# Three of the four products of the first layer's scale and shift in split float32r

## The chip, the cores and the metric

One core of one Trainium2 chip. The metric is the device time of one execution of the whole program in microseconds (us); the runs of the kernel before are given with their median.

## The reference, cut to what matters

Two layers of a diffusion backbone over 256 latent and 256 context tokens with 1024 features. Everything starts with a scale and a shift of the inputs, which come from a conditioning vector: one for the latent stream (`c`), one for the context stream (`c_ctx`).

```python
mod_l = (jax.nn.silu(c) @ lp['w_ada'] + lp['b_ada'])[:, None, :]
mod_c = jax.nn.silu(c_ctx) @ lp['w_ada'] + lp['b_ada']
sh1_l, sc1_l, g1_l, sh2_l, sc2_l, g2_l = jnp.split(mod_l, 6, axis=-1)
sh1_c, sc1_c, g1_c, sh2_c, sc2_c, g2_c = jnp.split(mod_c, 6, axis=-1)
hl = xl * (1 + sc1_l) + sh1_l
hc = xc * (1 + sc1_c) + sh1_c
pl = hl @ lp['w_in']
```

`w_ada` is 1024 x 6144 for each layer, `w_in` 1024 x 8704. For the first layer's first product, `sc1` and `sh1` of all 1024 features are needed, which are 2048 columns of `w_ada`.

## The kernel before, in words

Features lie on the 128 partitions, in 8 tiles of features; the 512 tokens of both streams lie side by side in the free dimension. Every large product is made of three float32r products: an operand is split into a high part (ScalarE rounds it to float32r, `split`, L155) and a low part (the rest, a subtraction on VectorE or, where told so, on GpSimd, `lo_of`, L152), and `mm3` (L162 to L164) adds high x high, high x low and low x high in PSUM. The weights come as a stream of blocks of 128 x 1024 (`wfetch`), each split into `whi` and `wlo`, tiles of which there are three each.

The program's start, in `run`, goes so:

- `c` and `c_ctx`, as columns (`cc`), go through silu.
- The scale (j = 1) and the shift (j = 0) of the first 512 features (half 0), then of the other 512 (half 1), come from `ada_half`, called four times in the order (1,0), (0,0), (1,1), (0,1), written here as (j, half). Each call has four pieces of weights of 128 x 2 x 512 (`adar`, 512 KB each, fetched in `ada_raw`). It takes two columns of `cc` as the stationary operand and lets a piece's 512 columns stream by in float32, over eight tiles of features: eight products, which the trace shows as 16 matmuls of L1205. The row of two streams x 512 is copied out of PSUM by ScalarE (`adarow`, L1207), turned into columns by four transposes (L1210), and VectorE adds the bias and writes `mod` (L1213).
- `first_h` makes the first product's moving operand from x, scale and shift: per tile of features and stream, ScalarE writes the high part `hh` (L1180), VectorE the exact value `hf` (L1182), and the low part `hl` is the difference, on VectorE for one stream and on GpSimd for the other. It is called once for each half of the features.
- The first three tiles of the first projection (`u`, stationary operands `wx`, `wx` and one `whi`) are begun with the first half of the features (`early_half`, 12 products a tile) and ended with the second half. The next tile is `uv`.

In between, the hyena filter's small network (`filter_hidden`, with a sine on VectorE and ScalarE) is worked on.

Order on each engine is set by a scheduler at build time, which places an instruction by the order of the program, by priority (`high_priority` moves the calls of `ada_half` and the second `first_h` ahead) and by free tiles. On the chip each engine then goes through its list in that order, and waits on semaphores. All fetches here are issued by SyncE.

Of the kernel before, what the change touches and what calls it, by code (L numbers as in the profile page):

```python
# [11 lines left out]
F32R = mybir.dt.float32r  # L12
I32 = mybir.dt.int32
AF = mybir.ActivationFunctionType
ALU = mybir.AluOpType
# [33 lines left out]
RS = -1024.0 / 27      # what the reciprocal square roots come multiplied with  # L49

# columns of the packed per-feature vectors of one layer
# [12 lines left out]
class Kernel:  # L64
# [48 lines left out]
    def pair(self, T, name):  # L113
        """high and low parts of [1024 features, T tokens]: one (hi, lo) for each tile of features"""
        if T == 512:
            a, b = self.big(F32R, name=name + "h"), self.big(F32R, name=name + "l")
            return [(a[:, k], b[:, k]) for k in range(KT)]
        t = self.big(F32R, [P, 2, KT, T], name=name)
        return [(t[:, 0, k], t[:, 1, k]) for k in range(KT)]

    # ---- work in the background: generators that go one step on after each tile of a projection,
    #      so that what a step waits for has been issued a tile earlier ----
# [43 lines left out]
    def mmx(self, out, a, b, start, stop):  # L166
        """as mm3, or one float32 product where the operands have not been split"""
        if isinstance(a, tuple):
            self.mm3(out, a, b, start, stop)
        else:  # L170
            self.nc.tensor.matmul(out, lhsT=a, rhs=b, start=start, stop=stop)
# [40 lines left out]
    def fill(self, n):  # L212
        """fetches up to n blocks of weights, and two more into a large tile"""
# [6 lines left out]
    def wblock(self, ahead=2):  # L220
        """the next block of the weight stream as (hi, lo); the blocks after it are asked for early"""
# [11 lines left out]
    def dense(self, h, T, name):  # L233
        """one tile of 128 output features: [P, T] in PSUM"""
# [12 lines left out]
    def dense_by_stream(self, h, T, n, name):  # L247
        """n tiles, all of one stream's products before the other's; the last stream goes by tile of features,
        as they come out of the normalisation"""
# [10 lines left out]
    def dense_by_feature(self, ws, os, h, c0, T):  # L260
        """several tiles at once, one tile of input features after the other"""
# [9 lines left out]
    def rsqrt(self, out, var, scale, shape, tag):  # L271
        """out = RS / sqrt(var * scale + EPS)"""
# [6 lines left out]
    def newton(self, x, a, t):  # L279
        """x = RS / sqrt(a): a seed from the exponent bits, a cubic step x' = x (r^2 - 10/3 r + 5) with r = a x^2,  # L280
        which leaves 8/3 times the next value, and a Newton step that takes it as it comes"""
# [14 lines left out]
    def sine(self, out, pre, b, freq):  # L296
        """out = sin(freq * (pre + b)), the argument brought into [-pi, pi]"""
# [12 lines left out]
    def bcast_cols(self, ps_out, cols):  # L310
        """ps_out[:, i*128+j] on every partition = cols[j, i] / D"""
# [7 lines left out]
    def filter_hidden(self, l):  # L319
        """hidden features of the filter's network, [HID, SEQ]: their high parts and, below, their low ones"""  # L320
# [24 lines left out]
    def start_filters(self, l):  # L345
        """starts the filters; self.inv: the inverse transform's table, [freq, parity, cos/sin, 128];
        self.fwd: the forward one's, [tok, (parity, cos/sin, 128)], in the first layer split into high and low parts"""
        if l == 0:
            self.specs = {}
            self.hyb = self.big(F32R, [P, 4, 2, 512], name="hyb")      # two filters' parts, the tokens', the table  # L350
# [7 lines left out]
    def filter_chain(self, l):  # L358
        """specs[quarter]: spectrum of the normalised filter plus the skip weight for 256 channels,
        [freq, freq tile, re/im, ch], and what is left to multiply with"""  # L360
# [18 lines left out]
    def filter_quarter(self, l, qd, wf, hk, spec):  # L379
        """The filter has its skip weight times its norm added to its first tap; its norm is divided out at the very end."""  # L380
# [8 lines left out]
        hk = v4(hk, "hk")                                      # [tok, fwd/bwd, parity, ch]  # L389
# [13 lines left out]
        sq = wf.rearrange("p (i c) -> p i c", i=4)           # its inputs are spent  # L403
# [5 lines left out]
        # per-channel norm, as columns  # L409
# [35 lines left out]
    def parts(self, dst, src, eng=None):  # L445
        """splits src [tok, parity, ch] into dst; returns the pair of parts for a parity"""
# [4 lines left out]
    def transform(self, l, out, zc, zs):  # L451
        """cosine sums of zc and sine sums of zs, both [tok, ch] by parity, into [freq, freq tile, cos/sin, ch].
        The second tile holds the frequencies mirrored: 255 - k, with the sine's sign turned."""
# [24 lines left out]
    def hyena_unit(self, l, qd, s, z, x0, hy):  # L478
        """long convolution of 256 channels of one stream"""
# [21 lines left out]
        y = next(self.ys)                                      # [freq, re/im, freq tile, ch]  # L501
# [5 lines left out]
        # what the even and what the odd tokens are made of  # L507
# [18 lines left out]
    def short_conv(self, l, u, ch, out, ns):  # L526
        """out = three-tap convolution along the tokens of each stream + bias"""
# [9 lines left out]
    def hyena(self, l, h, T):  # L537
        """units of the last quarter are left to what follows"""
# [26 lines left out]
    def pool_in(self, l, h, T, po):  # L565
        """window mean minus value, all channels"""
# [3 lines left out]
        for c in range(KT):  # L570
# [7 lines left out]
            # the sum of a window of `step` tokens; its range shrinks as the window grows  # L578
# [15 lines left out]
    def pool_out(self, l, po, T, half):  # L594
        """the groups' projections of one half of the channels, in place"""
# [82 lines left out]
    def keys(self, kf, sqs, kh):  # L678
        """normalises and rotates the keys, on the way into kh"""
# [31 lines left out]
    def query(self, hh, q, sq, qs, st, kh, vh, T):  # L711
        """the queries' norms, as columns; after a group of heads its rotation, and its heads are let go"""
# [24 lines left out]
    def head(self, hh, s, q, qs, kh, vh, T, shared):  # L737
        """attention of one head over one stream's queries; its output takes the queries' place"""
# [58 lines left out]
    def ln_tile_(self, st, m, o, eng=None):  # L797
        """tile m of the residual sum, o its product in PSUM. The deviations are taken from the
        mean of the first tile's features; the rest of the mean comes out at the end."""
# [35 lines left out]
    def ln_sums(self, st):  # L835
        """the sums over all but the last tile, on every partition"""
# [16 lines left out]
    def ln_finish_(self, st, outs, done=None, gap=1):  # L853
        """outs: (kind, destination, scale columns, shift columns), fed from the normalised value"""
# [3 lines left out]
        bc, a, t = st["bc"], st["acc"][:, 0], st["acc"][:, 1]      # the sums' place is free again  # L858
# [38 lines left out]
    def raw_pair(self, a, b):  # L897
        """high and low parts of a value before its normalisation, scaled by what follows it; two more columns: the scale, the shift"""
# [12 lines left out]
    def from_raw(self, o, rm):  # L911
        """the product with the normalised value from that with the raw one"""
# [8 lines left out]
    def fold(self, g, b, sc, sh):  # L921
        """(x*g+b)*sc+sh as one scale and one shift"""
# [68 lines left out]
    def layer(self, l, h, hc, xa):  # L991
# [74 lines left out]
        if ns == 1:  # L1066
# [4 lines left out]
            # the head of the next product goes by the raw value, so that it need not wait for the normalisation  # L1071
# [38 lines left out]
    def run(self):  # L1110
# [9 lines left out]
        th = self.const([P, KT, 2], "ccolt")  # L1120
        nc.scalar.activation(th, cc, AF.Tanh, scale=0.5)
        nc.vector.tensor_scalar(out=th, in0=th, scalar1=0.5, scalar2=0.5, op0=ALU.mult, op1=ALU.add)
        nc.vector.tensor_tensor(out=cc, in0=cc, in1=th, op=ALU.mult)
        x = self.big(F32, [P, KT, 512], name="x")
# [11 lines left out]
        # the first tiles of the first projection, from one half of their features after the other  # L1136
# [207 lines left out]
```

## Time and profile before

| | |
|---|---|
| time, median of 3 runs | 1757.83 us (1756.98 to 1757.92) |
| span of the profiled execution, first to last instruction | 1754.7 us |
| the median less that span | 3.1 us |
| TensorE busy | 1685.5 us, 96% of the span |
| VectorE, ScalarE, GpSimd busy | 1237.0, 711.8, 334.7 us |
| chain that ended last | PE 80%, DVE 12%, issue 3%, ACT 2%, POOL 1%, DMA 1% |

The profiled execution's own time is not given beyond its span; what lies around the span is taken as the difference to the median. PE is TensorE's matmuls, PEld its weight loads, DVE VectorE, ACT ScalarE, POOL GpSimd, SP SyncE. The chain is followed back from the last instruction to what released it. All that the change touches lies in the first 60 us.

### The profile page before, as it was taken

Reading aid. Unit: us, or ns where it says so; the run is one execution under the profiler, and the core shown is the slowest. Engines: PE = TensorE matmul, PEld = TensorE weight load, DVE = VectorE, ACT = ScalarE, POOL = GpSimd, SP = SyncE. Lnnn points to the kernel's source line nnn. Section 1 sums busy time; section 2 is a strip of 40 time slices with the busy share of each in tenths; the row PEclk is TensorE's granted clock in tenths of the full one; section 3 lists DMA queues with packets and bytes.
Section 4 is the critical chain, followed back from the end, with each engine's and each line's share of the span. In section 5 each row is a group of like instructions: output and inputs, shape, how many; then the busy total and the mean of one; then the engine's idle time right before and its main releaser. Section 6 shows DMA issues by size and latency. Waiting matters only on the chain.

```text
span 1754.7 us, 25630 instructions
## 1 busy us (share of the span) xinstructions
PE 1685.5 (96%) x9930; PEld 1458.4 (83%) x9930; DVE 1237.0 (70%) x2050; ACT 711.8 (41%) x1132; POOL 334.7 (19%) x314
## 2 busy tenths in 40 slices
PE   8999999999999999899999999989999999989996
PEld 2788887788888888788888877879899999979995
DVE  4778878655777765878865576499874785796665
ACT  3433333432454433342232222255353664554442
POOL 1143451001200000340000041156500210130011
PEclk9999999999999999999999999989999999999998
DMA  8422222444322344216666564134353535545552
GB/s 319 146 79 85 72 83 94 144 142 141 124 72 73 132 154 135 85 61 192 191 196 198 186 195 132 61 121 144 120 165 126 173 97 160 173 135 184 190 181 84
DMA packets 68769, 243.34 MB, mean 139 GB/s; under 512 B 8166, under 2 KB 8616, under 8 KB 68392
## 3 DMA queue, kind: packets, MB, share of 16 engines
q1 hardware_dynamic: 67192, 236.78, 41.2%
q0 software_dynamic: 1168, 4.72, 0.9%
q8 instruction: 78, 1.28, 0.3%
q14 instruction: 43, 0.35, 0.1%
q10 hardware_dynamic: 288, 0.21, 0.0%
HBM read 238.01 MB, written 1.05 MB: 136 GB/s over the span
## 4 chain that ended last, share of the span: by engine, by line
PE 80%; DVE 12%; issue 3%; ACT 2%; POOL 1%; DMA 1%; SPq 0%; ACTq 0%; DVEq 0%; POOLq 0%
PE f L163 7%; PE f L162 7%; PE f L164 7%; PE b L162 4%; PE b L163 4%; PE b L164 4%; PE g L164 4%; PE g L162 4%; PE g L163 4%; PE w L162 3%; PE w L164 3%; PE w L163 3%; DVE wlo L152 2%; PE ux L162 1%; PE q L162 1%
## 5 line engine op out<-in xcount | busy, mean ns | idle before, releaser
L155 ACT ACTIVATE whi<-raw 128x1024 fp32r<-128x1024 f32 x322 | 340.9, 1059 | 666.1 <-issue 128.5
L152 DVE TENSOR_TENSOR wlo<-raw,whi 128x1024 fp32r<-128x1024 f32 x311 | 400.1, 1287 | 218.0 <-ACT whi L155 216.5
L183 DVE SCALAR_TENSOR_TENSOR junk<-ada,silu 128x1024 bf16<-128x1024 f32 x128 | 158.3, 1237 | 79.4 <-DMA ada<-adat 78.5
L162 PE MATMUL f<-h2h,whi 128*128 128x512 f32 (+1 forms) x320 | 125.7, 393 | 0.9 <-DVE sg L957 0.9
L163 PE MATMUL f<-h2l,whi 128*128 128x512 f32 (+1 forms) x320 | 125.6, 393 | 0.0
L164 PE MATMUL f<-h2h,wlo 128*128 128x512 f32 (+1 forms) x320 | 125.6, 393 | 0.0
L829 POOL TENSOR_TENSOR y<-y,lncs 128x256 f32<-128x256 f32 (+2 forms) x12 | 21.7, 1836 | 419.9 <-ACT lncs L824 419.9
L162 PE MATMUL f<-h,whi 128*128 128x256 f32 x312 | 88.5, 284 | 6.7 <-DVE fraw L916 6.7
L162 PE MATMUL w<-a,whi 128*128 128x256 f32 (+1 forms) x284 | 90.8, 320 | 0.0
L164 PE MATMUL w<-a,wlo 128*128 128x256 f32 (+1 forms) x284 | 89.6, 315 | 0.0
L163 PE MATMUL w<-a,whi 128*128 128x256 f32 (+1 forms) x284 | 89.5, 315 | 0.0
L163 PE MATMUL f<-h,whi 128*128 128x256 f32 x312 | 88.3, 283 | 0.0
L164 PE MATMUL f<-h,wlo 128*128 128x256 f32 x312 | 88.2, 283 | 0.0
L164 PE MATMUL g<-hh,wlo 128*128 128x512 f32 x192 | 76.8, 400 | 0.0
L162 PE MATMUL g<-hh,whi 128*128 128x512 f32 x192 | 76.7, 399 | 0.0
L163 PE MATMUL g<-hl,whi 128*128 128x512 f32 x192 | 76.3, 398 | 0.0
L162 PEld LDWEIGHTS f<-h2h,whi 128*128 128x128 f32 x320 | 60.1, 188 | 15.2 <-DVE sg L957 1.1
L164 PEld LDWEIGHTS f<-h2h,wlo 128*128 128x128 f32 x320 | 60.1, 188 | 14.3
L163 PEld LDWEIGHTS f<-h2l,whi 128*128 128x128 f32 x320 | 60.1, 188 | 14.1
L162 PEld LDWEIGHTS f<-h,whi 128*128 128x128 f32 x312 | 59.4, 191 | 6.9 <-ACT y L895 6.9
L163 PEld LDWEIGHTS f<-h,whi 128*128 128x128 f32 x312 | 59.5, 191 | 0.0
L164 PEld LDWEIGHTS f<-h,wlo 128*128 128x128 f32 x312 | 59.4, 191 | 0.0
(478 smaller groups left out, 4990.8 us busy)
## 6 DMA issues: line engine op xcount, KB each, us to landing
raw<-wst SPq DMA_DIRECT2D x336, 512.0 KB, 3.6
ada<-adat SPq DMA_DIRECT2D x80, 512.0 KB, 3.9
adar<-ada SPq DMA_DIRECT2D x16, 512.0 KB, 10.2
qsw<-q POOLq DMA_DIRECT2D x16, 128.0 KB, 4.8
x<-x_t POOLq DMA_DIRECT2D x1, 2048.0 KB, 9.6
x<-x_t SPq DMA_DIRECT2D x1, 1024.0 KB, 11.4
x<-x_t SPq DMA_DIRECT2D x2, 512.0 KB, 10.2
silu<-c_row SPq DMA_DIRECT2D x2, 512.0 KB, 7.9
```

Of the source, the lines that this page charges most:

```text
L152: (eng or self.nc.vector).tensor_tensor(out=lo, in0=src, in1=hi.bitcast(F32), op=ALU.subtract)
L155: self.nc.scalar.activation(hi, src, AF.Copy)
L162: t.matmul(out, lhsT=ah, rhs=bh, start=start, stop=False)
L163: t.matmul(out, lhsT=ah, rhs=bl, start=False, stop=False)
L164: t.matmul(out, lhsT=al, rhs=bh, start=False, stop=stop)
L183: nc.vector.scalar_tensor_tensor(out=junk, in0=raw, scalar=1.0, in1=self.silu[:, s], op0=ALU.mult, op1=ALU.mult, accum_out=mod[:, s, m : m ...
L829: nc.gpsimd.tensor_tensor(out=y[:, a:b], in0=xa[:, a:b], in1=cb.to_broadcast([P, b - a, SEQ]), op=ALU.subtract)
```

## The change

Three of the four calls of `ada_half`, all but (1,0), get their weights split into float32r parts and a stationary operand of four columns: high parts of the two columns of `c` and their low parts (`ccolp`). Each of the eight tiles of features then takes two float32r matmuls (high and low part of the weights) instead of one float32 product. The four rows that come out are folded into two by the small products that turn rows into columns, whose moving operand is now `fold4` instead of a 2 x 2 identity; (1,0) uses `fold4` too, in its first two rows. The split pieces are `whi`/`wlo` tiles, from the same three of each as the weight stream's; of the four pieces of a call the third has its low part made on GpSimd, the others on VectorE. The small tile `ccolt` comes from the pool `t2`.

```diff
@@ run
-        th = self.const([P, KT, 2], "ccolt")
+        th = self.t2(name="ccolt")[:, : 2 * KT].rearrange("p (k s) -> p k s", s=2)
         nc.scalar.activation(th, cc, AF.Tanh, scale=0.5)
         nc.vector.tensor_scalar(out=th, in0=th, scalar1=0.5, scalar2=0.5, op0=ALU.mult, op1=ALU.add)
         nc.vector.tensor_tensor(out=cc, in0=cc, in1=th, op=ALU.mult)
+        cp = self.sb.tile([P, KT, 4], F32R, tag="ccolp", name="ccolp", bufs=1)
+        self.split(cp[:, :, 0:2], cp[:, :, 2:4], cc)
+        self.fold4 = self.const([4, 2], "fold4")
+        nc.vector.tensor_tensor(out=self.fold4, in0=self.ident[:4, 0:2], in1=self.ident[:4, 2:4], op=ALU.add)
+        cc = (cc, cp)
...
@@ ada_half
         o = self.aux(name="adar")
+        exact, parts = cc
+        n = 2 if (j, half) == (1, 0) else 4
         for kp in range(4):
+            if n == 2:
+                ws = (raws[kp],)
+            else:
+                ws = [self.sb.tile([P, 2, 512], F32R, tag=t, name=self.nm("a" + t), bufs=3) for t in ("whi", "wlo")]
+                self.split(*ws, raws[kp], nc.gpsimd if kp == 2 else None)
             for k in range(2):
-                nc.tensor.matmul(o[:2], lhsT=cc[:, 2 * kp + k], rhs=raws[kp][:, k], start=kp + k == 0, stop=kp + k == 4)
+                for i, w in enumerate(ws):
+                    nc.tensor.matmul(o[:n], lhsT=(exact if n == 2 else parts)[:, 2 * kp + k], rhs=w[:, k],
+                                     start=kp + k + i == 0, stop=kp + k == 4 and i == len(ws) - 1)
         row = self.t2(name="adarow")
-        nc.scalar.activation(row[:2], o[:2], AF.Copy)
+        nc.scalar.activation(row[:n], o[:n], AF.Copy)
         tp = self.aux([P, 4, 2], name="adat")
         for m in range(4):
-            nc.tensor.transpose(tp[:, m], row[:2, m * P : (m + 1) * P], self.ident[:2, :2])
+            nc.tensor.matmul(tp[:, m], lhsT=row[:n, m * P : (m + 1) * P], rhs=self.fold4[:n], start=True, stop=True)
```

Three places in the order of instructions matter. The first is TensorE's list from the filter's second product (`hf`) to the first product with a low part of the weights `wx`. Before:

```order
L336 MATMUL hf_25_163<-hf1h_134,hfs_92 128x256
L1205 MATMUL adar_249<-adar_220,ccol 2x512 x2
L1205 MATMUL adar_249<-adar_222,ccol 2x512 x2
L1205 MATMUL adar_249<-adar_224,ccol 2x512 x2
L1205 MATMUL adar_249<-adar_226,ccol 2x512 x2
L162 MATMUL u_234<-hh_88,wx_211 128x512
L163 MATMUL u_234<-hl_89,wx_211 128x512
L162 MATMUL u_235<-hh_88,wx_211 128x512
L163 MATMUL u_235<-hl_89,wx_211 128x512
L162 MATMUL u_236<-hh_88,whi_230 128x512
```

and in the change:

```order
L336 MATMUL hf_34_192<-hf1h_139,hfs_97 128x256
L162 MATMUL u_263<-hh_93,wx_240 128x512
L163 MATMUL u_263<-hl_94,wx_240 128x512
L162 MATMUL u_264<-hh_93,wx_240 128x512
L163 MATMUL u_264<-hl_94,wx_240 128x512
L164 MATMUL u_263<-hh_93,wx_240 128x512
```

The product of (1,1), four pieces, stood ahead of the first tiles of `u`, and that of (0,1) directly behind these five; now both come later, in parts, among the products of `u`.

The second place is VectorE's list from the low parts of the first two weight blocks (`wx`) to the second half's `hf`; `mod_72` is the scale, `mod_71` the shift. Before:

```order
L152 TENSOR_TENSOR wx_211<-raw_212,wx_211 128x1024
L1213 SCALAR_TENSOR_TENSOR mod_72<-adat_260,vecs 128x4 x2
L152 TENSOR_TENSOR wx_211<-raw_216,wx_211 128x1024
L1213 SCALAR_TENSOR_TENSOR mod_71<-adat_312,vecs 128x4 x2
L1182 TENSOR_SCALAR hf_325<-x_87,mod_72,mod_71 128x256
```

and in the change:

```order
L152 TENSOR_TENSOR wx_240<-raw_241,wx_240 128x1024
L152 TENSOR_TENSOR wx_240<-raw_245,wx_240 128x1024
L152 TENSOR_TENSOR awlo_280<-adar_249,awhi_279 128x1024
L152 TENSOR_TENSOR awlo_288<-adar_251,awhi_287 128x1024
L152 TENSOR_TENSOR awlo_304<-adar_255,awhi_303 128x1024
L152 TENSOR_TENSOR awlo_356<-adar_320,awhi_355 128x1024
L152 TENSOR_TENSOR awlo_364<-adar_322,awhi_363 128x1024
L1228 SCALAR_TENSOR_TENSOR mod_72<-adat_313,vecs 128x4 x2
L152 TENSOR_TENSOR awlo_380<-adar_326,awhi_379 128x1024
L152 TENSOR_TENSOR wlo_436<-raw_433,whi_435 128x1024
L152 TENSOR_TENSOR wlo_442<-raw_439,whi_441 128x1024
L1228 SCALAR_TENSOR_TENSOR mod_71<-adat_389,vecs 128x4 x2
```

Between the two low parts of `wx` and the second half's shift, eight more subtractions of 128 x 1024 stand on VectorE: six of `ada_half`, and two of the weight stream that stood behind the second half's `hf` before.

The third place is ScalarE's list from the last piece of (1,1) to the second half's `hh`. Before, the two copies of rows stood right behind the high part of the third weight block:

```order
L155 ACTIVATE whi_230<-raw_228 128x1024
L1207 ACTIVATE adarow_258<-adar_249 2x512
L1207 ACTIVATE adarow_310<-adar_301 2x512
L1180 ACTIVATE hh_88<-x_87,mod_71,mod_72 128x256 x8
L155 ACTIVATE hyb_90<-dftraw_320 128x512
```

and in the change:

```order
L155 ACTIVATE awhi_303<-adar_255 128x1024
L155 ACTIVATE awhi_355<-adar_320 128x1024
L155 ACTIVATE awhi_363<-adar_322 128x1024
L1222 ACTIVATE adarow_311<-adar_278 4x512
L155 ACTIVATE awhi_371<-adar_324 128x1024
L155 ACTIVATE awhi_379<-adar_326 128x1024
L155 ACTIVATE whi_435<-raw_433 128x1024
L155 ACTIVATE whi_441<-raw_439 128x1024
L1222 ACTIVATE adarow_387<-adar_354 4x512
L1185 ACTIVATE hh_93<-x_92,mod_71,mod_72 128x256 x8
```

Each copy of rows now stands behind two high parts of pieces that come after its product. From `uv` on, the order on every engine is the same as before.

## Rows read from the trace of the kernel before

**Rows 1.** The page's head, engines' busy time, the slices of TensorE, the chain by engine.

```profile
span 1754.7 us, 25630 instructions
...
PE 1685.5 (96%) x9930; PEld 1458.4 (83%) x9930; DVE 1237.0 (70%) x2050; ACT 711.8 (41%) x1132; POOL 334.7 (19%) x314
...
PE   8999999999999999899999999989999999989996
...
PE 80%; DVE 12%; issue 3%; ACT 2%; POOL 1%; DMA 1%; SPq 0%; ACTq 0%; DVEq 0%; POOLq 0%
```

**Rows 2.** Windows of the start: length, busy time and count per engine, TensorE clock, DMA.

```profile
17.20:24.20 7.00, 7.00 (x17) 1.25 (x16) 2.64 (x7) 1.70 (x2) 0.00 (x0) 1.00 1.02 409
...
25.80:32.80 7.00, 7.00 (x17) 1.28 (x17) 6.51 (x16) 7.00 (x13) 1.53 (x2) 1.00 1.02 409
...
47.00:60.00 13.00, 13.00 (x58) 10.55 (x57) 12.10 (x18) 10.39 (x15) 2.89 (x3) 1.00 0.58 201
```

**Rows 3.** Timeline of PE: start, duration, engine, line, operation, shapes, count, idle before.

```profile
25.21 0.70 PE L336 MATMUL hf<-hf1h,hfs 64*128 64x256 f32 x2
25.84 7.03 PE L1205 MATMUL adar<-adar,ccol 128*2 128x512 f32 x16
32.80 0.50 PE L162 MATMUL u<-hh,wx 128*128 128x512 f32 x1
...
41.85 0.50 PE L164 MATMUL u<-hh,wx 128*128 128x512 f32 x1
...
49.66 0.39 PE L162 MATMUL u<-hh,wx 128*128 128x512 f32 x1
...
57.73 0.40 PE L164 MATMUL u<-hh,wlo 128*128 128x512 f32 x1
57.97 0.40 PE L162 MATMUL uv<-hh,whi 128*128 128x512 f32 x1
```

**Rows 4.** Timeline of ACT, 15 to 33 us.

```profile
15.57 0.59 ACT L1207 ACTIVATE adarow<-adar 2x512 f32<-2x512 f32 x1 [12.36 <-PE adar L1205]
20.24 1.28 ACT L308 ACT_TABLE_LOAD   x1 [4.08 <-DVE sa L307]
21.53 0.42 ACT L308 ACTIVATE hf1h<-sa 64x256 f32<-64x256 f32 x1
24.24 0.59 ACT L1207 ACTIVATE adarow<-adar 2x512 f32<-2x512 f32 x1 [2.29 <-PE adar L1205]
...
30.17 1.99 ACT L155 ACTIVATE wx<-raw 128x1024 fp32r<-128x1024 f32 x2
```

**Rows 5.** Timeline of DVE, 25 to 53 us.

```profile
25.32 0.23 DVE L1213 SCALAR_TENSOR_TENSOR mod<-adat,vecs 128x4 f32<-128x4 f32 x2 [5.19 <-PE adat L1210]
...
34.61 1.74 DVE L152 TENSOR_TENSOR wx<-raw,wx 128x1024 fp32r<-128x1024 f32 x1
...
36.42 3.22 DVE L152 TENSOR_TENSOR wx<-raw,wx 128x1024 fp32r<-128x1024 f32 x1
...
43.42 0.23 DVE L1213 SCALAR_TENSOR_TENSOR mod<-adat,vecs 128x4 f32<-128x4 f32 x2 [3.79 <-PE adat L1210]
...
48.51 0.41 DVE L152 TENSOR_TENSOR hl<-hf,hh 128x256 fp32r<-128x256 f32 x1
...
49.99 2.35 DVE L152 TENSOR_TENSOR wlo<-raw,whi 128x1024 fp32r<-128x1024 f32 x2
```

**Rows 6.** Timeline of POOL beside DVE, at 35 us and at 1187 us.

```profile
35.23 3.32 POOL L152 TENSOR_TENSOR wlo<-raw,whi 128x1024 fp32r<-128x1024 f32 x1
...
1187.46 2.39 POOL L152 TENSOR_TENSOR wlo<-raw,whi 128x1024 fp32r<-128x1024 f32 x1
```

**Rows 7.** Windows around an idle stretch of TensorE (columns as in Rows 2).

```profile
1276.00:1281.00 5.00, 0.96 (x9) 0.75 (x7) 4.33 (x9) 1.35 (x3) 0.80 (x6) 0.95 0.50 170
1281.00:1284.00 3.00, 3.00 (x14) 3.00 (x15) 2.35 (x7) 0.77 (x2) 0.00 (x0) 0.51 0.19 74
1284.00:1287.00 3.00, 3.00 (x27) 3.00 (x27) 2.46 (x5) 1.44 (x4) 0.41 (x2) 1.00 0.21 44
```

**Rows 8.** Timeline of PE at that idle stretch.

```profile
1281.00 2.07 PE L519 MATMUL yt<-dfts,zf 128*128 128x128 f32 x8 [4.04 <-DVE hyy L521]
```

## Prediction

> **What bounds the kernel now.** I read the page first: TensorE is busy for 96% of the span, eight or nine tenths in every slice, and holds 80% of the chain that ended last [rows 1]. A microsecond taken from or added to TensorE's work before the first projection is therefore a microsecond of the whole, unless something else takes TensorE's place. So the second view is a table of windows over the start: TensorE is busy for all of 17.2 to 24.2, of 25.8 to 32.8 and of 47 to 60 us [rows 2]. The third is TensorE's timeline. The float32 product of one call of `ada_half` is 16 matmuls in 7.03 us; the first matmul of `u` starts at 32.80, the first that needs a low part of `wx` at 41.85, the second half of `u` at 49.66, and `uv`, from which on the order is unchanged, at 57.97 [rows 3]. That last number is the one to forecast.
>
> The fourth view is what runs beside it. While TensorE did (1,1), ScalarE and VectorE made the first half of h and the parts of `wx`: ScalarE has both high parts at 32.2, VectorE the low parts at 36.35 and 39.64 [rows 4, 5]. While it did (0,1), from 34.89 to 41.92, those low parts came out unnoticed. The slow float32 products cover work that TensorE would else wait for.
>
> **The change, part by part.** *TensorE's work.* Float32r matmuls of 512 columns follow each other every 0.231 us: the 36 of the second half lie between 49.66 and 57.97, and 8.31 / 36 = 0.231 [rows 3]. That a stationary operand of 4 columns streams as fast as one of 128 I take from the float32 product, where the columns passing by set the pace too. Sixteen make 3.7 us instead of 7.03, so 3.3 us less in each of three calls, 9.9 in all.
>
> *Added work.* Each of 12 pieces costs ScalarE 1.0 us (1.99 for two) [rows 4]; nine cost VectorE 1.15 to 1.22 (2.35 for two) [rows 5]; three cost GpSimd 2.39 where nothing holds it up [rows 6]. GpSimd's subtraction at 35.23 took 3.32, and VectorE's at 36.42 beside it 3.22 instead of 1.2, ending 1.1 after GpSimd's [rows 5, 6]: VectorE stood until GpSimd was done. I let them exclude each other below.
>
> *(0,0).* Its pieces land before 15 us, and two are split while TensorE does (1,0). The other two high parts stand behind the copy at 15.57 [rows 4], to 16.8 and 18.9; GpSimd's low part runs from 16.8 to 19.2 and holds the sine's steps on VectorE, into which the last low part is put as well. So TensorE ends this product near 22.9 instead of 24.2, but the copy of its row now stands on ScalarE behind the sine's table load and activation (1.28 + 0.42 [rows 4]), and the sine's argument comes at 22.6 instead of 20.2. That gives 24.4 for the copy (24.24 before), and `mod` at 25.65 (25.55 before, [rows 5]). Worth nothing. The first fetches go out some 0.4 us earlier, which ends in the same wait.
>
> *First half of h, `wx`.* The same instructions behind a `mod` 0.1 later: low parts of `wx` at 36.5 and 39.75 [rows 5]. TensorE now has nothing from 26 to 31.6, does four matmuls, and stops at the first low part until 36.5. It has lost the cover.
>
> *(1,1) and (0,1).* One of the three `whi`/`wlo` tiles is held by the third weight block until the end of `u`, so pieces go in pairs: a third piece's high part waits for TensorE's last matmul on the first. From 39.75: low parts of pieces 1 and 2 at 40.9 and 42.1; TensorE, with nine matmuls of `u` in its list ahead, is done with piece 1 at 42.7; high part of piece 3 to 43.8, its low part on GpSimd to 46.2; VectorE's low part of piece 4, held by it, to 47.3; product done at 48.7. The copy of the row stands behind two high parts of (0,1), which wait for the tiles of pieces 3 and 4: 50.3; transposes and `mod` 51.2. (0,1) repeats it: low parts of pieces 1 and 2 at 50.8, tiles free at 51.6, high part 52.7, GpSimd 55.1, VectorE 56.5, product done at 57.5. Ahead of its copy stand the high parts of two blocks of the weight stream, 2.0 us: copy at 59.1, second shift at 60.1, where it was 43.65 [rows 5].
>
> *Second half.* From shift to the last low part of h took 48.92 - 43.42 = 5.5 us [rows 5]; GpSimd's and TensorE's order make it 6.3, so 66.4. Behind the last `hl` stand 21 matmuls, 4.9 us: `uv` at 71.4 instead of 57.97, **13.5 us later**. Before, 36 matmuls of the first half were still left when the shift came, so that only part of the wait was seen; now none are.
>
> *The clock.* After the idle 4.04 us that end at 1281 [rows 8], the granted clock was 0.51 for 3 us and then 1.00 [rows 7], that is 1.2 and then 2.4 GHz. The idle stretches before 36.5, 5.6 and over 3 us, are like it; ten matmuls at half rate then end 2.3 us later, of which 1.0 fills a wait for the second `wx`: **1.3 us**.
>
> The Trainium skill, TensorE: Matmul & The Clock Gate, section on HAM oscillation, says more: gaps between bursts bring the lower clock back again and again. No run here shows it for a stretch of this kind. By that rule the whole stretch to 60 us, half idle, would run at the lower clock, `uv` would come at 78.4 and the sum would be +20.4 instead of +14.8; rows 7 show a single return to full clock, and I go by the rows.
>
> *Sum.* 13.5 + 1.3 = +14.8 us; nothing behind `uv` catches it up, since TensorE is busy to eight or nine tenths there [rows 1]. The span 1754.7 becomes 1769.5; the median stands 3.1 over the span, so the time is 1757.8 + 14.8 = **1772.6 us**. The bounds: without any exclusion of VectorE and GpSimd, and at full clock, the same steps give `uv` at 66.3 (+8.4, 1766.2); at half clock throughout +20.4 (1778.2).
>
> **The rivals.** *The cover holds* (the other side). TensorE stays the bound, and the 9.9 us go: 1747.9. This needs the second shift before the first half's 36 matmuls and the two shorter products are done: 36 x 0.231 + 7.4 = 15.7 us after TensorE can go on, 36.5 + 15.7 = 52.2. By VectorE's list alone, eight subtractions of 1.15 after 39.75 come to 49 us, so it would have to run without a single wait. For it: TensorE's share of the chain [rows 1]. Against it: the pairs of tiles, and the copies behind high parts. By the Trainium skill, FP8 and Floating Point Precision, TensorE Precision Notes, true FP32 is four passes; that would make the saving 3.7 us a call, 1746.7; no row here counts passes, and 7.03 against 3.7 us is 1.9 for two matmuls against one.
>
> *No exclusion.* VectorE and GpSimd overlap freely, and the low parts of `wx` come at 33.6 and 34.8: 1766. Against it, VectorE's 1.2 us that took 3.22 beside GpSimd [rows 5, 6].
>
> *Low clock throughout.* Some 30 matmuls that the steps above wait for take 0.23 us more each, 6.9: 1778. TensorE is about half busy from 36 to 60 us; rows 7 show the return to full clock only under solid work.
>
> *Caught up later.* The delay is taken back in the first projection, because weights and filter parts lie ready early: within 0.2%. Against it, TensorE's busy slices [rows 1].
>
> **How the numbers follow.** Forecast, within 4 us of 1772.6: 0.60. No exclusion: 0.14. Low clock: 0.17. Cover holds: 0.05. Caught up: 0.04. The range takes in both bounds and 1 to 2 us for handovers that I did not count: 1764 to 1779. A change of 0.2%, 3.5 us, is about what a measurement of this kernel can tell from none; so faster 0.05, same 0.04, slower 0.91.
>
> **What would show it.** Right: TensorE idle for some 5 us before the first `u` and again before its first low-part matmul; the second shift near 60 us; `uv` near 72.8; TensorE's busy time lower by under 10 us while the span grows; ScalarE waiting for TensorE before the third and fourth high parts. Wrong: `mod` of (0,0) well before 25 us, a second shift before 52 us, or `uv` before 62 us.

## The result, and the profile after

The change is slower: 1774.34 us (median of 4 runs, 1773.12 to 1774.38) against 1757.4 us of the kernel before beside it (4 runs, 1753.75 to 1757.92), ratio 1.0104 with a 95% interval of 1.0092 to 1.0117. The forecast was 1772.6. The page of the changed kernel, with the lines that answer to [rows 1]; PEclk is the granted TensorE clock by slices, in tenths:

```profile
span 1772.5 us, 25707 instructions
...
PE 1687.3 (95%) x9946; PEld 1467.2 (83%) x9946; DVE 1254.7 (71%) x2061; ACT 723.7 (41%) x1145; POOL 342.2 (19%) x317
...
PE   5899999999999999989999999989899999989996
...
PEclk7999999999999999999999999989999999989998
...
PE 80%; DVE 12%; issue 3%; ACT 1%; POOL 1%; ACTq 0%; DVEq 0%; POOLq 0%
```

The first slice (44 us) fell from eight tenths to five, the second from nine to eight, and the rest differs in three slices by one tenth: the loss lies in the start. The chain's shares moved by a per cent at most, so the page alone would not have told. TensorE's busy time did not fall, though its products of `ada_half` became shorter. The table of windows shows where it stands and at which clock (length, busy time and count of PE, PEld, DVE, ACT, POOL, then clock and DMA):

```profile
17.00:25.00 8.00, 4.74 (x20) 1.52 (x20) 4.91 (x10) 3.24 (x4) 2.27 (x1) 0.92 1.03 409
25.00:33.00 8.00, 2.75 (x10) 2.02 (x10) 5.10 (x15) 5.66 (x12) 0.77 (x1) 0.50 1.02 408
33.00:37.00 4.00, 2.17 (x4) 1.00 (x4) 4.00 (x9) 3.83 (x5) 2.23 (x3) 0.50 0.17 65
37.00:44.00 7.00, 5.77 (x14) 4.32 (x15) 6.75 (x4) 0.00 (x0) 3.40 (x2) 0.50 0.43 132
44.00:55.00 11.00, 9.67 (x46) 5.79 (x45) 5.07 (x5) 4.72 (x5) 2.37 (x1) 0.99 0.68 255
55.00:65.00 10.00, 5.27 (x25) 2.37 (x24) 6.52 (x10) 6.02 (x8) 2.61 (x2) 0.98 0.19 56
65.00:70.00 5.00, 5.00 (x16) 3.79 (x16) 4.99 (x9) 4.97 (x10) 2.91 (x4) 0.69 0.39 120
```

Where TensorE was busy throughout at full clock before [rows 2], it now works for 2.75 of 8 us, and its clock is 0.50 (1.2 GHz) from 25 to 44 us and 0.69 in the mean from 65 to 70. TensorE's timeline:

```profile
17.45 0.39 PE L1219 MATMUL adar<-awhi,ccolp 128*4 128x512 f32 x1
17.68 0.40 PE L1219 MATMUL adar<-awlo,ccolp 128*4 128x512 f32 x1
...
24.74 1.86 PE L1225 MATMUL adat<-fold,adarow 4*128 4x2 f32 x8 [2.06 <-ACT adarow L1222]
...
33.10 0.79 PE L162 MATMUL u<-hh,wx 128*128 128x512 f32 x1 [5.34 <-ACT wx L155]
...
38.23 0.80 PE L164 MATMUL u<-hh,wx 128*128 128x512 f32 x1 [2.96 <-DVE wx L152]
...
49.71 0.39 PE L1219 MATMUL adar<-awlo,ccolp 128*4 128x512 f32 x1 [1.33 <-POOL awlo L152]
...
58.95 0.39 PE L1219 MATMUL adar<-awlo,ccolp 128*4 128x512 f32 x1 [1.96 <-POOL awlo L152]
...
74.69 0.40 PE L162 MATMUL uv<-hh,whi 128*128 128x512 f32 x1
```

`uv` starts 16.7 us later than in [rows 3], nearly the whole loss (the medians differ by 16.9 us, the ratio makes it 18.3). Every wait of TensorE in between is for ScalarE, VectorE or GpSimd. ScalarE, which has the third and fourth high part of (1,1) to make, waits 9 us for TensorE to let go of the first two pieces:

```profile
46.10 2.22 ACT L155 ACTIVATE awhi<-adar 128x1024 fp32r<-128x1024 f32 x2 [9.27 <-PE adar L1219]
```

VectorE's timeline:

```profile
26.64 0.23 DVE L1228 SCALAR_TENSOR_TENSOR mod<-adat,vecs 128x4 f32<-128x4 f32 x2 [4.22 <-PE adat L1225]
...
36.43 5.05 DVE L152 TENSOR_TENSOR wx<-raw,wx 128x1024 fp32r<-128x1024 f32 x2
41.40 2.35 DVE L152 TENSOR_TENSOR awlo<-adar,awhi 128x1024 fp32r<-128x1024 f32 x2
48.35 2.39 DVE L152 TENSOR_TENSOR awlo<-adar,awhi 128x1024 fp32r<-128x1024 f32 x1 [4.60 <-ACT awhi L155]
...
54.63 0.23 DVE L1228 SCALAR_TENSOR_TENSOR mod<-adat,vecs 128x4 f32<-128x4 f32 x2 [0.54 <-PE adat L1225]
57.45 2.53 DVE L152 TENSOR_TENSOR awlo<-adar,awhi 128x1024 fp32r<-128x1024 f32 x1 [2.59 <-ACT awhi L155]
...
63.37 0.23 DVE L1228 SCALAR_TENSOR_TENSOR mod<-adat,vecs 128x4 f32<-128x4 f32 x2 [0.26 <-PE adat L1225]
```

And GpSimd's:

```profile
47.29 2.37 POOL L152 TENSOR_TENSOR awlo<-adar,awhi 128x1024 fp32r<-128x1024 f32 x1 [6.89 <-PE adar L1219]
...
56.55 2.35 POOL L152 TENSOR_TENSOR awlo<-adar,awhi 128x1024 fp32r<-128x1024 f32 x1 [6.89 <-ACT awhi L155]
```

VectorE's subtraction at 48.35 takes 2.39 us, and ends 1.1 after GpSimd's (49.66); two in a row without GpSimd take 2.35. The second shift comes at 63.37 instead of 43.42 [rows 5].

### The profile page after: what moved, and what is told of

The parts are those of the page before. It is cut to its first block, busy times and chain, and to the rows that moved or that the text cites. A ratio compares the mean times of both kernels' runs of the same rounds, so it can differ in the third digit from the quotient of the medians.

```text
span 1772.5 us, 25707 instructions
## 1 busy us (share of the span) xinstructions
PE 1687.3 (95%) x9946; PEld 1467.2 (83%) x9946; DVE 1254.7 (71%) x2061; ACT 723.7 (41%) x1145; POOL 342.2 (19%) x317
## 3 DMA queue, kind: packets, MB, share of 16 engines
HBM read 238.01 MB, written 1.05 MB: 135 GB/s over the span
## 4 chain that ended last, share of the span: by engine, by line
PE 80%; DVE 12%; issue 3%; ACT 1%; POOL 1%; ACTq 0%; DVEq 0%; POOLq 0%
PE f L162 6%; PE f L163 6%; PE f L164 6%; PE b L162 4%; PE b L163 4%; PE b L164 4%; PE g L164 4%; PE g L163 4%; PE g L162 4%; PE w L162 3%; PE w L164 3%; PE w L163 3%; DVE wlo L152 2%; PE ux L162 2%; PE ux L164 1%
## 5 line engine op out<-in xcount | busy, mean ns | idle before, releaser
L162 PEld LDWEIGHTS f<-h2h,whi 128*128 128x128 f32 x320 | 60.1, 188 | 15.4 <-DVE sg L957 1.1
L164 PEld LDWEIGHTS f<-h2h,wlo 128*128 128x128 f32 x320 | 60.1, 188 | 14.1
L163 PEld LDWEIGHTS f<-h2l,whi 128*128 128x128 f32 x320 | 60.1, 188 | 14.1
L163 PEld LDWEIGHTS f<-h,whi 128*128 128x128 f32 x312 | 60.1, 193 | 0.0
L164 PEld LDWEIGHTS f<-h,wlo 128*128 128x128 f32 x312 | 60.1, 193 | 0.0
```

What stands on the lines that cost most here:

```text
L162: t.matmul(out, lhsT=ah, rhs=bh, start=start, stop=False)
L163: t.matmul(out, lhsT=ah, rhs=bl, start=False, stop=False)
L164: t.matmul(out, lhsT=al, rhs=bh, start=False, stop=stop)
```

## The experiments

Ratios are to the kernel before, run on the same chip as the experiment; times of different experiments are in part from different chips and are compared by these ratios. 0.001 is 1.76 us. Each ratio has an interval of 0.0009 to 0.0017 to either side, so two of them are told apart from a difference of some 0.002 on. Each edit is to the changed kernel, and the scheduler sets the order of instructions anew for it, so the order can differ too. The theory was that the shorter products are worth nothing, because VectorE sets when TensorE can go on; the subtractions for the split stand in line on VectorE and GpSimd, and with the cover of the slow products gone TensorE waits for them and loses its clock.

**One call split at a time.** In the place of `n = 2 if (j, half) == (1, 0) else 4`:

```diff
+        n = 4 if (j, half) == (0, 0) else 2
```

> Only the call (0,0) is split, the other three stay float32 products. Theory (the loss comes from the splits that stand in a row on VectorE, GpSimd and ScalarE in the calls (1,1) and (0,1), and from the cover that TensorE's work gave): within 1.5 us of the kernel before, since the copy of the row stands behind the sine's activation on ScalarE; second shift within 1.5 us of 43.4 us. Rival A (TensorE's work is what counts): 3.3 us faster. Rival B (each split call costs alike, a third of the loss): 5.6 us slower.

Measured: 1762.56 us, ratio 1.0044 (1.0029 to 1.0059).

```diff
+        n = 4 if (j, half) == (1, 1) else 2
```

> Only the call (1,1) is split. Theory: the largest part, 8 to 12 us slower than before, since TensorE idles from 26 to 31 us and from 33 to 36 us, and the second shift's float32 product can start only when the split scale is done, near 50 us. Rival A (TensorE's work counts): 3.3 us faster. Rival B (alike): 5.6 us slower.

Measured: 1769.22 us, ratio 1.0080 (1.0064 to 1.0097).

```diff
+        n = 4 if (j, half) == (0, 1) else 2
```

> Only the call (0,1) is split. Theory: 2 to 5 us slower than before; TensorE is covered until 33 us by the float32 product of (1,1), then waits for low parts; second shift near 49 us. Rival A (TensorE's work counts): 3.3 us faster. Rival B (alike): 5.6 us slower.

Measured: 1762.62 us, ratio 1.0047 (1.0032 to 1.0062).

By the ratios that is 7.7 us for (0,0), 14.0 for (1,1) and 8.3 for (0,1). All three also contain the fold in place of the transposes, which costs 3.3 us alone, as the next run but one shows; less that, 4.4, 10.7 and 4.9 are left. Each part alone is slower, (1,1) by far the most: its split keeps the product from being done while ScalarE and VectorE make the first half of h, and TensorE idles 5.35 us there. The call (0,0) alone is not free, as the theory had it. Its `mod` came late (26.53 instead of 25.32), and the two float32 products behind it were slow. TensorE's timeline of the kernel with (0,0) split:

```profile
27.57 8.32 PE L1219 MATMUL adar<-adar,ccol 128*2 128x512 f32 x16
...
38.12 0.50 PE L164 MATMUL u<-hh,wx 128*128 128x512 f32 x1 [1.56 <-DVE wx L152]
39.02 1.05 PE L1225 MATMUL adat<-fold,adarow 2*128 2x2 f32 x8
39.99 8.72 PE L1219 MATMUL adar<-adar,ccol 128*2 128x512 f32 x16
```

Besides the clock (8.32 and 8.72 instead of 7.03), the row of (1,1) is folded behind a matmul that waits for `wx`, where it stood ahead of it before.

**Shorter products without a split.** No call is split, and two of four pieces of the three calls are left out. The fold stands in place of the transposes, as in the change:

```diff
-        n = 2 if (j, half) == (1, 0) else 4
+        n = 2
-        for kp in range(4):
+        for kp in (range(4) if (j, half) == (1, 0) else (0, 3)):
```

> All calls are float32 products as before, but the calls (0,0), (1,1) and (0,1) leave out two of their four pieces of weights: TensorE does 3.5 us less in each, close to what the split products save, and nothing is split. Theory: the saving is there to be had when nothing is added, 5 to 10 us faster than before. Rival C (the first projection waits for the parts of wx and h whatever TensorE does, so a shorter product is worth nothing): within 2 us of before.

Measured: 1758.22 us, ratio 1.0016 (1.0007 to 1.0025).

**The fold alone.** No call is split:

```diff
-        n = 2 if (j, half) == (1, 0) else 4
+        n = 2
```

> The kernel before, with the four transposes of each call replaced by products with the fold matrix, as in the change, and no piece split. Theory (the split alone makes the loss; a fold in place of the transposes takes 0.64 us longer, of which the first halves' four calls are mostly covered): 0.5 to 1.5 us over before, about 1758.5. Rival (the fold carries a good part of the loss): 4 us or more over before.

Measured: 1759.54 us, ratio 1.0019 (1.0010 to 1.0029), 3.3 us, more than the 0.5 to 1.5 expected. TensorE's timeline of the kernel before, with the four transposes of (0,0) and the product of (0,1):

```profile
24.88 0.41 PE L1210 MATMUL adat<-ident,adarow 2*128 2x2 f32 x4 [0.68 <-ACT adarow L1207]
...
34.89 7.03 PE L1205 MATMUL adar<-adar,ccol 128*2 128x512 f32 x16
```

and of the fold alone:

```profile
24.89 1.05 PE L1225 MATMUL adat<-fold,adarow 2*128 2x2 f32 x8 [0.67 <-ACT adarow L1222]
...
26.49 8.72 PE L1219 MATMUL adar<-adar,ccol 128*2 128x512 f32 x16
```

The fold takes 1.05 us where the four transposes took 0.41, and in this execution the clock fell behind it (8.72 instead of 7.03), which is 1.7 of the 3.3 us. The run with half of the work has this fold too. It takes some 3.5 us of TensorE's work out of each of three calls, and its ratio is the same as that of the fold alone. So the shorter products were worth nothing that can be measured, even where they cost nothing: the theory's 5 to 10 us missed, and the rival that the product's time is not what bounds the start holds. The timeline of the run with half of the work says what does:

```profile
25.62 1.88 PE L1219 MATMUL adar<-adar,ccol 128*2 128x512 f32 x4
31.04 0.50 PE L162 MATMUL u<-hh,wx 128*128 128x512 f32 x1 [3.54 <-ACT wx L155]
...
32.71 3.05 PE L1219 MATMUL adar<-adar,ccol 128*2 128x512 f32 x4
36.17 0.50 PE L164 MATMUL u<-hh,wx 128*128 128x512 f32 x1 [0.41 <-DVE wx L152]
```

TensorE waits for the parts of `wx`, which stand on ScalarE and VectorE behind the first half of h, for 4.2 us of what it saved. The rest went otherwise. TensorE's list is not that of the fold alone with less in it: the last piece of (1,1) stands behind three matmuls of `u` and ran at a low clock (32.71, 3.05 us instead of 1.88), and between the two pieces of (0,1) stand 14 matmuls of `u`, so that the second shift came at 48.00, where the fold alone has it at 46.65. What half of the products would be worth in the order of before is not shown.

**No low part on GpSimd.**

```diff
-                self.split(*ws, raws[kp], nc.gpsimd if kp == 2 else None)
+                self.split(*ws, raws[kp])
```

> The change, with every low part of the pieces on VectorE, none on GpSimd. Theory (GpSimd's 2.4 us hold VectorE off, so that two low parts cost 3.7 us instead of 2.4): 1.2 to 2 us earlier in each of (1,1) and (0,1), uv 3 to 4 us earlier, time about 1770.5. Rival (VectorE and GpSimd run beside each other): 0 to 2 us slower than the change, since VectorE has one subtraction more in each call.

Measured: 1769.49 us, ratio 1.0080 (1.0065 to 1.0095), 4.2 us under the change by the ratios and 4.9 by the medians. On VectorE the two last low parts of (1,1) now take 2.39 together, where one took that beside GpSimd, and the second shift comes 4.3 us earlier:

```profile
45.51 2.39 DVE L152 TENSOR_TENSOR awlo<-adar,awhi 128x1024 fp32r<-128x1024 f32 x2 [1.66 <-ACT awhi L155]
...
59.11 0.23 DVE L1228 SCALAR_TENSOR_TENSOR mod<-adat,vecs 128x4 f32<-128x4 f32 x2 [0.36 <-PE adat L1225]
```

Help from GpSimd costs here instead of helping. That VectorE stands beside GpSimd is shown: its one subtraction at 48.35 in the change took 2.39 us and ended 1.1 after GpSimd's. The Trainium skill, SBUF — State Buffer, section on the two separate sides of SBUF, has it that a VectorE operation with two inputs in SBUF and a GpSimd operation that reads SBUF lock each other out for a whole instruction; these 2.39 us agree. But the 4 us can't be put down to the exclusion. TensorE's timeline of the change has the first matmuls on VectorE's two held low parts:

```profile
51.10 0.40 PE L1219 MATMUL adar<-awlo,ccolp 128*4 128x512 f32 x1
...
60.03 0.39 PE L1219 MATMUL adar<-awlo,ccolp 128*4 128x512 f32 x1
```

The held low parts were ready at 50.74 and 59.98, so TensorE came to the first without a wait and lost 0.16 us on the second. Its two waits there, 1.33 and 1.96 us, end with GpSimd's own subtraction, which takes 2.37 where VectorE's takes 1.2. Most of the gain is therefore that a slow subtraction left TensorE's path. No run has the one without the other.

**No low parts at all.**

```diff
-                ws = [self.sb.tile([P, 2, 512], F32R, tag=t, name=self.nm("a" + t), bufs=3) for t in ("whi", "wlo")]
-                self.split(*ws, raws[kp], nc.gpsimd if kp == 2 else None)
+                ws = [self.sb.tile([P, 2, 512], F32R, tag="whi", name=self.nm("awhi"), bufs=3)]
+                nc.scalar.activation(ws[0], raws[kp], AF.Copy)
```

> The change without the low parts of the pieces: 12 subtractions (nine on VectorE, three on GpSimd) and the 24 matmuls that stream them are left out, so that three of the four products are those of the weights' high parts alone; ScalarE's high parts, the pairs of tiles, the copies and the fold stay. Theory (VectorE's and GpSimd's subtractions are the larger part of the loss behind the second low part of wx): second shift at 52 to 56 us instead of 63.4, time 1763 to 1768, 6 to 11 us under the change. Rival (tiles, the copies behind high parts and the lower clock hold the products as long): within 3 us of the change. Were all of the loss in the low parts, the time would be that of the run with the fold alone, 1759.

Measured: 1762.47 us, ratio 1.0035 (1.0022 to 1.0049), 12 us under the change. VectorE's timeline of it:

```profile
47.18 0.23 DVE L1228 SCALAR_TENSOR_TENSOR mod<-adat,vecs 128x4 f32<-128x4 f32 x2 [8.13 <-PE adat L1225]
52.24 0.23 DVE L1228 SCALAR_TENSOR_TENSOR mod<-adat,vecs 128x4 f32<-128x4 f32 x2 [4.83 <-PE adat L1225]
```

The second shift is at 52.24, where the theory had 52 to 56, though the pairs of tiles and a fallen clock (0.50 around 33 to 37 us) are still there. ScalarE's order is not quite that of the change:

```profile
50.52 0.59 ACT L1222 ACTIVATE adarow<-adar 4x512 f32<-4x512 f32 x1 [0.71 <-PE adar L1219]
...
56.91 1.99 ACT L155 ACTIVATE whi<-raw 128x1024 fp32r<-128x1024 f32 x2
```

The high parts of two blocks of the weight stream, which stood ahead of the second copy, now come behind it, and one high part of (0,1) stands ahead of the first copy instead of two. In the change the two copies start 0.78 and 0.77 us after their products end, here 0.15 and 0.04; up to 1.4 of the 12 us belong to that. The twelve subtractions, with the 24 matmuls that need them, are still the larger part of the loss, some 10.7 of 18.3 us. What is left over before, 0.0035, is 0.0016 more than the fold alone, at the edge of what can be told apart.

**The clock.** 24 float32r matmuls whose product nobody reads stand ahead of the first `u`:

```diff
+        with self.tc.high_priority(500):
+            o = self.aux(name="warm")
+            for i in range(24):
+                nc.tensor.matmul(o[:4], lhsT=cp[:, 0], rhs=h[0][0], start=i == 0, stop=i == 23)
```

> The change, with 24 float32r matmuls of 512 columns added whose product nobody reads, in TensorE's list between the filter network's second product and the first matmul of u; they need only the first tile of h and fill the idle stretch before 33 us. Theory (the lower clock from 24.7 to 43.9 us is a term of its own): granted clock 1.00 from about 32 us on, the third high part of (1,1) is released some 3 us earlier, uv near 71.5 instead of 74.7, time about 1771, 2 to 5 us under the change. Rival (the clock costs nothing, all waits are for VectorE, GpSimd and tiles): within 1 us of the change, 1774. Rival B (the added matmuls are in the way): slower than the change.

Measured: 1775.59 us, ratio 1.0116 (1.0099 to 1.0133): no gain. Windows of it:

```profile
44.00:55.00 11.00, 9.67 (x46) 5.28 (x45) 5.34 (x6) 5.52 (x6) 2.37 (x1) 1.00 0.75 274
55.00:65.00 10.00, 5.47 (x20) 2.75 (x19) 6.62 (x10) 5.24 (x8) 2.62 (x2) 0.69 0.27 69
65.00:70.00 5.00, 5.00 (x14) 3.72 (x14) 4.98 (x9) 4.97 (x10) 2.89 (x4) 0.61 0.25 94
```

The clock was full from 33 to 55 us, and the second scale came 1.2 us earlier (53.42), but then it fell longer than in the change (0.69 and 0.61 against 0.98 and 0.69), and the second half of `u` lost what had been won. So a second run fills the later stretches too:

```diff
+        if n == 4 and j == 0:
+            d = self.aux(name="warm")
+            for i in range(8):
+                nc.tensor.matmul(d[:4], lhsT=parts[:, 0], rhs=ws[1][:, i % 2], start=i == 0, stop=i == 7)
...
+        if (j, half) == (0, 1):
+            d = self.aux(name="warm")
+            for i in range(6):
+                nc.tensor.matmul(d[:4], lhsT=parts[:, 0], rhs=ws[1][:, i % 2], start=i == 0, stop=i == 5)
```

> The change with 46 float32r matmuls added whose products nobody reads: 8 behind the product of (0,0), 24 ahead of the first matmul of u, 8 behind the product of (0,1), 6 behind its fold, so that TensorE works through the idle stretches. Theory (the lower clock costs what it takes from the matmuls that others wait for: fold of (0,0) 0.8, u and the pieces of (1,1) 1.2 as the run with 24 showed, fold and first u of the second half 2): granted clock near 1.00 from 17 to 75 us, uv near 71, time 1770 to 1771.5. Rival (what TensorE loses at the lower clock is waiting time anyway): within 1 us of the change, 1774.3.

Measured: 1771.22 us, ratio 1.0085 (1.0073 to 1.0097), 3.3 us under the change by the ratios. Windows of it:

```profile
17.00:25.00 8.00, 8.00 (x32) 3.12 (x32) 4.89 (x10) 3.37 (x5) 2.36 (x1) 0.79 1.03 410
25.00:33.00 8.00, 7.25 (x29) 2.93 (x27) 5.70 (x16) 6.67 (x13) 0.78 (x1) 0.79 1.03 409
...
55.00:65.00 10.00, 9.00 (x41) 4.75 (x41) 7.37 (x14) 6.83 (x12) 2.78 (x4) 1.00 0.17 53
65.00:70.00 5.00, 4.40 (x18) 3.22 (x18) 5.00 (x8) 4.26 (x7) 1.82 (x2) 1.00 0.33 110
```

With full clock from 33 us to the end of the start some 3 us come back, by a difference of ratios (0.0019) that is just clear of the noise. The clock may cost more than that in the change, since it was not full before 33 us here and the added matmuls take time themselves.

**Transposes instead of the fold.**

```diff
-        tp = self.aux([P, 4, 2], name="adat")
+        tp = self.aux([P, 4, n], name="adat")
...
-            nc.tensor.matmul(tp[:, m], lhsT=row[:n, m * P : (m + 1) * P], rhs=self.fold4[:n], start=True, stop=True)
+            nc.tensor.transpose(tp[:, m], row[:n, m * P : (m + 1) * P], self.ident[:n, :n])
...
+            if n == 4:
+                nc.vector.tensor_tensor(out=self.mod[0][j][:, s, c : c + 4], in0=tp[:, :, 2 + s], in1=self.mod[0][j][:, s, c : c + 4], op=ALU.add)
```

> The change with transposes of the rows in place of the products with the fold matrix, high and low products then added on VectorE by two more instructions of 128 by 4. Theory (the fold is a part of the loss of its own, 0.64 us in each call at full clock and more at the lower one; the run with the fold alone was 3.4 us over before): 2 to 3.5 us under the change, 1771 to 1772. Rival (in the changed kernel the copies and the second addition take its place): within 1 us of the change.

Measured: 1773.16 us, ratio 1.0102 (1.0087 to 1.0117), not to be told from the change. Without GpSimd as well (both edits):

> As the run with transposes, and no low part of the pieces on GpSimd. Theory (two separate parts of the loss, 5 us for GpSimd as measured and 2 to 3.5 for the fold): 1766 to 1767.5. What then is left over before, some 11 us, is the splitting itself. Rival (they overlap): 1769, as without GpSimd alone.

Measured: 1769.98 us, ratio 1.0076 (1.0063 to 1.0089), not to be told from 1.0080 without GpSimd alone. In both profiled executions `uv` started 1.5 us earlier than in the kernel with the fold (73.15 against 74.69, 68.82 against 70.26), but the medians do not bear it out. The theory's 2 to 3.5 us were 0.0011 to 0.0020 of the time, too little to be told with certainty by these ratios: the fold is a loss by itself, and whether it is a separate one within the change stays open.

**Tiles of their own.** The first two pieces of each call get their parts in a table's place that is free here:

```diff
-                ws = [self.sb.tile([P, 2, 512], F32R, tag=t, name=self.nm("a" + t), bufs=3) for t in ("whi", "wlo")]
+                ws = [self.hyb[:, 2 * kp + i] if kp < 2 else self.sb.tile([P, 2, 512], F32R, tag=t, name=self.nm("a" + t), bufs=3) for i, t in enumerate(("whi", "wlo"))]
```

> The change, with the parts of the first two pieces of each call in a table's place that lies idle here, so that all four pieces have tiles of their own. Theory (the pieces go in pairs because of the weight stream's three tiles, and ScalarE's third high part waits 9 us for TensorE): third and fourth high parts of (1,1) before 42 us instead of 46.1, product near 47 to 49 instead of 51.9, second shift near 57 to 60 instead of 63.4, uv 4 to 6 us earlier, time 1768 to 1771. Rival (VectorE's subtractions and TensorE's list set the pace, not the tiles): within 1.5 us of the change.

Measured: 1775.11 us, ratio 1.0112 (1.0097 to 1.0127). It does not decide. With free tiles the scheduler put pieces of (1,1) ahead of the first half of h on ScalarE and VectorE, and the low parts of `wx` came 6.3 us later. Of these, 4.2 had arisen at (0,0) already, whose `mod` came at 30.79 instead of 26.64. VectorE's timeline of it:

```profile
34.51 1.22 DVE L152 TENSOR_TENSOR hyb<-adar,hyb 128x1024 fp32r<-128x1024 f32 x1
...
42.75 5.07 DVE L152 TENSOR_TENSOR wx<-raw,wx 128x1024 fp32r<-128x1024 f32 x2
47.74 3.36 DVE L152 TENSOR_TENSOR awlo<-adar,awhi 128x1024 fp32r<-128x1024 f32 x1
```

The third and fourth high parts were indeed made from 40.99 on instead of 46.1, and the product was still no earlier: TensorE waited 4.31 us for GpSimd's low part. What the pairs cost at an unchanged order stays open. No version tried here is faster than the kernel before.

## Why the prediction was right, and where it was off

Sign, place and size came out: +16.9 us by the medians (18.3 by the ratio), forecast +14.8, and the range held it. At `uv` the forecast was 1.9 us short (72.8, measured 74.69), and two terms were too small, as the steps show. By its steps:

- **TensorE's work.** Float32r matmuls with four columns follow each other every 0.23 us at full clock (17.45, 17.68), as forecast. But the sign "busy time lower" was wrong: it rose by 1.8 us. Up to `uv` TensorE was busy for 49.90 us before and 49.98 after. The products of `ada_half` took 8.5 us less (21.80 instead of 30.32), the folds 3.4 more than the transposes (5.01 instead of 1.59), and most of the rest is matmuls at 1.2 GHz, which last longer. The other 1.7 us lie behind `uv`.
- **(0,0), "worth nothing".** This step failed. Product at 22.7 (forecast 22.9) and copy at 24.1 (24.4) were right, yet `mod` was done at 26.87 instead of 25.65. The four fold products, eight matmuls, took 1.86 us at half clock, where the prediction had left the 0.41 of the transposes. It goes on counting transposes and never costs the fold, in this call or the others. Alone the fold is worth 3.3 us; with (0,0) split as well the loss is 7.7 by the ratio (6.3 by the medians, 1762.56 against 1756.26), so some 4 us are left for the split of (0,0) itself, where the forecast had nothing.
- **First half of h, `wx`.** TensorE idle before the first `u` (5.34 us) and again before the first low part (2.96): the lost cover, as forecast. The low parts took 5.05 us as in [rows 5], but from 36.43, so that they were ready at 41.48, forecast 39.75.
- **(1,1) and (0,1).** Copies behind high parts, high parts behind TensorE (9.27 us), VectorE held by GpSimd: all there. The second scale was done at 54.86 (forecast 51.2), the second shift at 63.60 (60.1). Between them lie 8.7 us, where the forecast has 8.9; the lag of 3.7 us had arisen before. TensorE was done with the first piece of (1,1) when ScalarE could go on, at 46.10, forecast 42.7: 1.7 of these 3.4 us are the later low parts of `wx`, and the rest is TensorE, which went at half clock until 44 us through the matmuls of `u` that stand ahead of that piece.
- **Second half.** From the shift to `uv` 11.1 us, forecast 11.3, although the clock fell once more between 65 and 68 us. Two counts are wrong without entering the sum. When the second shift came in the kernel before, 27 matmuls of the first half were left, not 36, and TensorE had no idle time until the second half, so none of the wait was seen there. And the 36 matmuls in "the cover holds" include four that were done by 36.5 by the prediction's own steps; with 32 its limit is 51.3 us instead of 52.2.
- **The clock, "1.3 us".** The other term that was too small. Half clock lasted from 25 to 44 us, over the first 17 matmuls of `u`, where the prediction counts ten, and came back for a second stretch; with TensorE kept busy from 33 us on, 3.3 us come back. The prediction took the one return in [rows 7], behind an idle stretch followed by solid work, as the rule; here TensorE got only pieces of work. The Trainium skill, TensorE: Matmul & The Clock Gate, section on HAM oscillation, says that gaps bring the lower clock back again and again; the two stretches agree with it in kind. The price that shows, 3.3 us, is about half of the 6.9 that the prediction estimates for half clock throughout; from 44 to 65 us the clock was nearly full (0.99 and 0.98).
- **Exclusion.** VectorE stands as forecast: one subtraction took 2.39 and 2.53 us, the two of `wx` 5.05. The 4.2 us that come back without GpSimd are mostly GpSimd's own slower subtraction on TensorE's path.

Of the rivals, "the cover holds" had no gain to offer at all: a start with shorter products and no split is no faster than the fold alone, in the order that it was given. "Low clock throughout" was half true. "No exclusion" is refuted by VectorE's 2.39 and 5.05 us, "caught up later" by the later slices of the page. What makes up the loss, by the runs that undo a part: low parts 12 us, up to 1.4 of them by the order of ScalarE, and GpSimd's 4.2 contained in them; the clock some 3, partly through the waits for the same low parts; the fold 3.3 by itself, but nothing measurable within the change. These overlap and are not to be added: the three calls split alone cost 0.0044, 0.0080 and 0.0047, and with the fold counted once that makes 0.0133, where the whole change cost 0.0104.

## What to carry to other kernels

A slow product on the busiest engine is no cost where it covers work that the same engine must wait for next; before it is shortened, take the work out of it without adding any (here half of its pieces), see whether the end moves, and look whether the order of instructions stayed. If the end doesn't move, what a faster form needs on the engines behind the wait comes on top: here nine subtractions on VectorE and three on GpSimd, with the matmuls that need them, cost some 11 us, to take 10 us off products whose shortening gained nothing. Cost the small products too, at the clock at which they will run.

## What the runs showed of the hardware

- The granted clock can stay at 0.50 for long under broken work: for 19 us, in the last seven of which TensorE was busy 5.77 us. It can also be low in a window in which TensorE has no idle time: 0.79 from 17 to 25 us with 8.00 us busy (the kernel with all stretches filled), and a float32 product of 16 matmuls without a gap took 8.72 instead of 7.03 in the kernel with the fold alone. The same product of (0,0) in the changed kernel ran from 17.45 at full pace, so where the clock falls is not the same in every execution.
- Small float32 products are dear: 4 products with 2 columns, as 8 matmuls, took 1.05 us at full clock and 1.86 at half, where 4 transposes of the same rows took 0.41.
- Per product, float32 costs 0.88 us (7.03 / 8) against 0.231 for float32r of the same 512 columns, 3.8 times. The Trainium skill, FP8 and Floating Point Precision, TensorE Precision Notes, speaks of four passes for true FP32, which is near 3.8; no run here counts passes.
